# Two SwiGLU feed-forwards of a decoder layer, their products made by seven block products in place of eight

## The chip, the cores and the metric

The kernel runs on one core of a Trainium2 chip. A core has TensorE (matrix products, into PSUM), VectorE and ScalarE (element-wise work, both can read PSUM), GpSimd (element-wise work in SBUF only) and SyncE, whose queue (SP) issues nearly all of this kernel's DMA transfers. In the profile they are PE (with PEld for its weight loads), ACT for ScalarE, DVE for VectorE, POOL for GpSimd and SP. The metric is the device time of one execution in microseconds; the median of several runs is compared.

## The reference

One layer of a hybrid decoder, for 1024 tokens of a prompt and 8 sequences of 8 new tokens. Model width 1024, feed-forward width 2816, all in float32. What concerns the change are the two half-step feed-forwards, one ahead of the token mixing and one behind it:

```python
def rmsnorm(x, g):
    xf = x.astype(jnp.float32)
    y = xf * lax.rsqrt(jnp.mean(xf * xf, axis=-1, keepdims=True) + EPS)
    return (y * g.astype(jnp.float32)).astype(x.dtype)

def swiglu(x, w_in, w_out):
    gu = x @ w_in                               # (tokens, 1024) @ (1024, 5632)
    g, u = gu[..., :D_FF], gu[..., D_FF:]
    return (jax.nn.silu(g) * u) @ w_out         # (tokens, 2816) @ (2816, 1024)

def layer(x, ...):
    x = x + 0.5 * swiglu(rmsnorm(x, norm_ffn1[l]), ffn1_w_in[l], ffn1_w_out[l])
    mix, ... = token_mixing(rmsnorm(x, norm_mix[l]), ...)
    x = x + mix
    x = x + 0.5 * swiglu(rmsnorm(x, norm_ffn2[l]), ffn2_w_in[l], ffn2_w_out[l])
```

The mixing (a causal pooling branch and a Mamba-2 state-space branch, merged by gates) is not changed in what it computes. At the end a final RMS norm gives the outputs; the states of the mixer are returned too.

## The kernel before

**Layout and precision.** Activations are feature-major: a tile has 128 features on the partitions and the tokens along it. The 1088 tokens are two halves, 512 tokens (half 0) and 576 (half 1: 512 of the prompt and the 64 new ones). A PSUM bank holds 512 columns, so half 1 is worked in two pieces of 288 (`PIECES`, L33). A product in float32 is made of three passes in a reduced float format: each operand is split into a high part and the exact rest, and high x high, high x low and low x high are added up (`products`, L252). So each pair of a weight block and a k-tile is nine matmuls: three passes of 512, 288 and 288 columns.

**Weights.** `load_w` (L239) loads up to four 128x128 blocks in one transfer (tile `wraw`, four buffers), ScalarE copies them to the high part `wh` (L248), VectorE subtracts to get the low part `wl` (L249); four buffers each. These splits have a raised priority.

**A feed-forward** (`ffn`, L391) goes through the 22 hidden tiles in blocks (`FF_BLOCKS`, L35: 3, 4, 4, 4, 4, 3). For each tile of a block: the gate product (`pg`, 8 k-tiles), SiLU, the up product (`pu`), their product, and a split into hidden high and low parts (`hb`, `hs`), which stay in SBUF. Then the block's share of the output product is made for all eight output tiles (`po`), and VectorE adds half of it to x straight from PSUM (L431). In the first block the two halves are worked one after the other, so that half 1's operand may still be made while half 0 is multiplied; in the last block the output runs by parts (`ends`, L391), so that the next stage can begin on what is finished. x stays in SBUF through the feed-forward.

**Ahead of the first feed-forward** `load_x` (L443) loads x token-major, turns it on TensorE, copies it from PSUM (L466, ScalarE and VectorE in turn) and splits x times its gain at once; the RMS factors are worked out beside the first products and applied to the product's result (`rs`). Elsewhere `norm_split` (L344) makes the normalized operand: squares, a sum over the partitions on TensorE, Newton steps, a way through DRAM to spread the factors (`rstd`, L303), the product, and one split for each of the eight tiles.

**Order.** Such helpers are generators, "chains". Each `yield` says how much TensorE time should pass before its next step, and `tick` (L132) weaves due steps into the stream of products; `finish` (L128) runs one to its end. The order so traced is each instruction's priority; what is issued first on each engine and on the DMA queue is then settled ahead of time by a scheduler that takes the first ready instruction by priority.

**Buffers.** 58 activation tiles of 128x576 (`act`, L82) are shared by all stages; three big tiles, small tiles and PSUM (four banks of products, four others) are opened once for the whole kernel.

**The end.** `turn_out` (L1152) turns finished blocks of 128 tokens to token-major, with ScalarE squaring and summing (L1159); `final` (L1177) scales and stores them. The last part has 256 prompt tokens and the 64 new ones (`parts`, L1150).

## Time and profile before

| what | us |
|---|---|
| runs | 3079.87, 3076.58, 3070.76 |
| median of the runs | 3076.58 |
| span of the profiled execution | 3076.2 |
| TensorE busy in it | 3024.0 (18600 matmuls) |
| VectorE busy | 1624.1 |
| ScalarE busy | 1028.7 |
| GpSimd busy | 56.4 |
| first feed-forward, first to last product | 12.4 to 831.6 |
| second feed-forward | 2268.0 to 3061.5 |

A row of the groups reads: line of the code, engine, operation, output tile <- input tiles, shape of each, how often, then busy time in us and mean ns of one, then the idle time of the engine just before them and what ended it. A row of a timeline or of the chain reads: start in us, length in us, engine, line, operation, count. A row of windows gives the stretch, its length, the busy time (and count) of each engine, the granted TensorE clock as a share of the full one, the busy share of the DMA engines, and GB/s. Matmuls are pipelined, so the duration of one is not its pitch: the pitch is the distance from start to start in a stretch that runs without idle time.

### The profile page before, as it was taken

How to read it: one execution, taken by the hardware profiler on the slowest of the kernel's cores; microseconds unless marked ns; L12 is line 12 of the kernel's file. 1: busy time of each engine (PE TensorE's matmuls, PEld its weight loads, DVE VectorE, ACT ScalarE, POOL GpSimd, SP SyncE). 2: the span in 40 equal slices, each digit the busy share in tenths (PEclk: the TensorE clock that was granted, in tenths of full speed). 3: DMA queues.
4: the chain of work that ended last, by engine and by line, in shares of the span. 5: the costliest groups of instructions: out<-in, count | busy, mean ns of one | idle time of the engine just before them, and what ended most of it. 6: DMA issues, size and time to landing. Idle time of an engine off the chain costs nothing.

```text
span 3076.2 us, 46636 instructions
## 1 busy us (share of the span) xinstructions
PE 3024.0 (98%) x18600; PEld 2750.7 (89%) x18600; DVE 1624.1 (53%) x3331; ACT 1028.7 (33%) x1967; POOL 56.4 (2%) x170
## 2 busy tenths in 40 slices
PE   6999999999999999999999999999999999999998
PEld 5999999999888888888999989999999999999997
DVE  5533333333673897777726886977773222322225
ACT  4221212121343665434425554543442212111113
POOL 0000000000000000000001110100000000000000
PEclk8999999999999999999999999999999999999999
DMA  4211111111434333435333434244432111111112
GB/s 132 67 45 45 45 45 45 45 45 43 130 97 124 113 103 92 117 117 183 91 102 95 123 104 119 88 139 124 145 113 64 44 45 45 45 45 45 45 41 98
DMA packets 439262, 261.10 MB, mean 85 GB/s; under 512 B 21795, under 2 KB 412066, under 8 KB 439036
## 3 DMA queue, kind: packets, MB, share of 16 engines
q1 hardware_dynamic: 439028, 258.11, 28.8%
q8 instruction: 146, 2.39, 0.3%
q14 instruction: 72, 0.59, 0.1%
q10 hardware_dynamic: 16, 0.00, 0.0%
HBM read 232.31 MB, written 25.97 MB: 84 GB/s over the span
## 4 chain that ended last, share of the span: by engine, by line
PE 92%; DVE 4%; DMA 2%; ACT 1%; issue 1%; SPq 0%; POOL 0%; ACTq 0%; DVEq 0%; POOLq 0%
PE pg L140 22%; PE pu L140 20%; PE po L140 17%; PE pc L140 8%; PE pz L140 6%; PE pso L140 5%; PE pwo L140 3%; PE pbp L140 3%; PE pyd L140 2%; PE pyos L140 1%; PE pst L140 1%; DMA bsel<-in_bsel_dram 1%; PE pyo L140 1%; PE pgm L140 1%; DVE wl L249 1%
## 5 line engine op out<-in xcount | busy, mean ns | idle before, releaser
L248 ACT ACTIVATE wh<-wraw 128x512 fp32r<-128x512 f32 (+1 forms) x708 | 440.2, 623 | 1643.8 <-PE pg L140 423.7
L249 DVE TENSOR_TENSOR wl<-wraw,wh 128x512 fp32r<-128x512 f32 (+1 forms) x708 | 479.1, 679 | 651.5 <-ACT wh L248 642.0
L140 PE MATMUL pg<-hi,wh 128*128 128x288 f32 (+1 forms) x1440 | 349.3, 331 | 15.4 <-ACT wh L248 15.4
L140 PE MATMUL po<-hb,wh 128*128 128x288 f32 (+2 forms) x1600 | 348.1, 339 | 0.0
L140 PE MATMUL pg<-lo,wh 128*128 128x288 f32 (+1 forms) x1440 | 346.3, 329 | 0.4 <-DVE lo L290 0.4
L140 PE MATMUL pg<-hi,wl 128*128 128x288 f32 (+1 forms) x1440 | 345.7, 328 | 0.0
L140 PE MATMUL pu<-hi,wh 128*128 128x288 f32 (+1 forms) x1248 | 293.9, 329 | 0.1
L140 PE MATMUL pu<-hi,wl 128*128 128x288 f32 (+1 forms) x1248 | 292.3, 328 | 0.0
L140 PE MATMUL pu<-lo,wh 128*128 128x288 f32 (+1 forms) x1248 | 292.2, 327 | 0.0
L140 PEld LDWEIGHTS pg<-hi,wh 128*128 128x128 f32 x1440 | 245.4, 189 | 38.0 <-ACT wh L248 16.3
L140 PEld LDWEIGHTS po<-hb,wh 128*128 128x128 f32 x1600 | 255.8, 188 | 19.6 <-ACT hb L286 0.3
L140 PEld LDWEIGHTS pg<-lo,wh 128*128 128x128 f32 x1440 | 245.3, 189 | 21.2 <-DVE lo L290 1.1
L140 PEld LDWEIGHTS pg<-hi,wl 128*128 128x128 f32 x1440 | 245.1, 189 | 20.7 <-DVE wl L249 0.4
L140 PE MATMUL po<-hb,wl 128*128 128x288 f32 (+3 forms) x1056 | 240.4, 328 | 0.0
L140 PEld LDWEIGHTS pu<-hi,wh 128*128 128x128 f32 x1248 | 211.8, 188 | 18.6 <-ACT wh L248 0.5
L140 PEld LDWEIGHTS pu<-hi,wl 128*128 128x128 f32 x1248 | 211.7, 188 | 17.7
L140 PEld LDWEIGHTS pu<-lo,wh 128*128 128x128 f32 x1248 | 211.7, 188 | 17.5
L140 PEld LDWEIGHTS po<-hb,wl 128*128 128x128 f32 x1056 | 178.6, 188 | 15.1
L431 DVE SCALAR_TENSOR_TENSOR x<-po,x 128x288 f32<-128x288 f32 (+3 forms) x240 | 108.7, 497 | 135.2 <-PE po L140 135.0
L140 PE MATMUL pc<-hi,wh 128*128 128x288 f32 (+1 forms) x576 | 162.8, 335 | 0.6 <-ACT craw L529 0.6
L140 PE MATMUL pc<-hi,wl 128*128 128x288 f32 (+1 forms) x576 | 159.7, 329 | 0.0
L140 PE MATMUL pc<-lo,wh 128*128 128x288 f32 (+1 forms) x576 | 158.6, 329 | 0.0
(283 smaller groups left out, 4608.6 us busy)
## 6 DMA issues: line engine op xcount, KB each, us to landing
wraw<-in_w_in_dram SPq DMA_DIRECT2D x260, 256.0 KB
wraw<-in_ffn_w_in_dram SPq DMA_DIRECT2D x200, 256.0 KB
wraw<-in_ffn_w_out_dram SPq DMA_DIRECT2D x64, 256.0 KB
ab<-acsd SPq DMA_DIRECT2D x64, 256.0 KB
wraw<-in_ssd_w_out_dram SPq DMA_DIRECT2D x64, 256.0 KB
wraw<-in_ffn_w_out_dram SPq DMA_DIRECT2D x48, 192.0 KB
wraw<-in_pool_w_out_dram SPq DMA_DIRECT2D x32, 256.0 KB
wraw<-in_w_o_dram SPq DMA_DIRECT2D x32, 256.0 KB
```

Source lines behind the costliest of these rows:

```text
L140: T.matmul(out, lhsT, rhs, start=start, stop=stop)
L248: S.activation(wh, raw, AF.Copy)
L249: V.tensor_tensor(wl, raw, wh.bitcast(F32), op=ALU.subtract)
L431: V.scalar_tensor_tensor(x_[:, a:b], pt[:, : b - a], 0.5, x_[:, a:b], op0=ALU.mult, op1=ALU.add)
```

## The change

Both products of both feed-forwards are made by one level of Strassen's scheme in Winograd's form. The two operands are cut into 2x2 blocks; seven sums and differences of blocks of each are formed, seven products are made of them in place of eight, and the four blocks of the result are sums of those.

- *Blocks.* Of the activations: two groups of k-tiles by two groups of tokens (256 + 256 in half 0, 288 + 288 in half 1, `NPAIR`). Of the input weights: the k-halves (4 + 4 tiles) by gate and up columns of one hidden tile. Of the output weights: the two halves of a block's hidden tiles by two neighbouring output tiles.
- *Operands.* GpSimd forms the sums (`combine` for activations, `add` in `wino_weights`). Each of the seven is split into high and low parts: `split_x` for activations (one activation tile holds both parts, 28 tiles for an operand of one half), `parts` for weights. The weights are loaded as before but combined anew for each use.
- *Accumulation.* `PRODUCTS` gives the order and the PSUM bank (0, 1 or 2) of the seven products; some add on to a bank that has been read in between. The result is put together on the way out of PSUM: by ScalarE, VectorE and GpSimd in `ffn_in` and `ffn_out`.
- *Order of the feed-forward.* All 22 hidden tiles are made first and stored to DRAM (`hdram`), the first three (`N_APART`) for each half by itself. Then, block by block (6, 6, 6, 4), the hidden tiles are loaded back, combined, and multiplied; x is stored ahead and loaded back for the sum.
- *Start.* `load_x` works out the RMS factors from the token-major x and makes the normalized, combined operand itself; all copies of turned blocks go to VectorE.
- *Buffers.* Raw weights 6 (4 before), split weights 3 (4), PSUM in the feed-forwards 6 banks of products and 2 others; pools for the stages open and close with each of the two feed-forwards and the mixer.
- *End.* The last part has half 1's five token blocks.

The diff, cut to its core (removed lines only where they aren't told above):

```diff
+NPAIR = (256, 288)
+FF_BLOCKS = (6, 6, 6, 4)
+N_RAW, N_W = 6, 3
+N_X2, N_TMP, N_S, N_PDF = 12, 11, 4, 6
+N_APART = 3
+PRODUCTS = (("1", 0), ("2", 1), ("6", 0), ("5", 2), ("7", 0), ("3", 2), ("4", 0))
...
+    def wino_weights(w, ka, kb, nk, ca, cb, raws=None):
+        if raws is None:
+            raws = wino_raw(w, ka, kb, nk, ca, cb)
+        a11, a12, a21, a22 = raws
+        def add(a, b, op, name):
+            t = stage["p"].tile([P, 4 * P], F32, tag="wsum", bufs=N_S, name=nm(name))[:, : nk * P]
+            with tc.high_priority(hp[0]):
+                G.tensor_tensor(t, a, b, op=op)
+            return t
+        def parts(a):
+            wh, wl = (sp.tile([P, 4 * P], F32R, tag=t, bufs=N_W, name=nm(t))[:, : nk * P] for t in ("wh", "wl"))
+            with tc.high_priority(hp[0]):
+                S.activation(wh, a, AF.Copy)
+                V.tensor_tensor(wl, a, wh.bitcast(F32), op=ALU.subtract)
+            return wh.rearrange("p (k c) -> p k c", c=P), wl.rearrange("p (k c) -> p k c", c=P)
+        yield parts(a11)
+        yield parts(a12)
+        s1 = add(a21, a22, ALU.add, "s1")
+        s2 = add(s1, a11, ALU.subtract, "s2")
+        yield parts(s2)
+        yield parts(s1)
+        s3 = add(a11, a21, ALU.subtract, "s3")
+        yield parts(s3)
+        s4 = add(a12, s2, ALU.subtract, "s4")
+        yield parts(s4)
+        yield parts(a22)
+    def wino(weights, nk, xs, after):
+        banks = [[None] * 3 for _ in xs]
+        for (p, b), (wh, wl) in zip(PRODUCTS, weights):
+            for i, (h, X) in enumerate(xs):
+                n = NPAIR[h]
+                new = banks[i][b] is None
+                if new:
+                    banks[i][b] = psum("pd", "pw" + p)
+                out = banks[i][b][:, :n]
+                for k in range(nk):
+                    x = X[p][k]
+                    for j, (W, c) in enumerate(((wh, 0), (wh, n), (wl, 0))):
+                        mm(out, W[:, k, :], x[:, c : c + n], start=new and k == 0 and j == 0, stop=k == nk - 1 and j == 2, free=True)
+                after(p, i, banks[i])
+                tick()
+    def split_x(src, h):
+        n = NPAIR[h]
+        t = act((P, 576), F32R, "X")
+        S.activation(t[:, :n], src, AF.Copy)
+        V.tensor_tensor(t[:, n : 2 * n], src, t[:, :n].bitcast(F32), op=ALU.subtract)
+        return t
+    def combine(h, pairs, X, pace=None):
...
+        for p, _ in PRODUCTS:
+            X[p] = []
+            for i, (a, b) in enumerate(pairs):
+                a1, a2, b1, b2 = a[:, :n], a[:, n : 2 * n], b[:, :n], b[:, n : 2 * n]
+                if p == "6":
+                    sub(a2, a2, a1)
+                    t2[i] = tmp(n, "t2")
+                    sub(t2[i], b2, a2)
+                elif p == "7":
+                    sub(a1, t2[i], a1)
+                elif p == "4":
+                    sub(b1, b1, t2[i])
+                X[p].append(split_x({"1": a1, "2": b1, "6": t2[i], "5": a2, "7": a1, "3": b2, "4": b1}[p], h))
+                if pace is not None:
+                    yield pace
+    def ffn_in(wi, ff, xs, hd, raws=None):
...
+            if p == "1":
+                out[i] = o = {"g": x2(name="g"), "t1": tmp(n)}
+                S.copy(o["t1"], A)
+                return
...
+            if p == "2":
+                V.tensor_tensor(g1, B, o["t1"], op=ALU.add)
+                S.activation(g1, g1, AF.Silu)
+            elif p == "6":
+                o["t2"] = tmp(n)
+                S.copy(o["t2"], A)
+            elif p == "5":
+                o["t5"] = tmp(n)
+                S.copy(o["t5"], C)
+            elif p == "7":
+                V.tensor_tensor(o["t5"], A, o["t5"], op=ALU.add)
+            elif p == "3":
+                V.tensor_tensor(g2, C, o["t2"], op=ALU.add)
+                S.activation(g2, g2, AF.Silu)
+            else:
+                V.tensor_tensor(g1, g1, A, op=ALU.mult)
+                G.tensor_tensor(g2, g2, o["t5"], op=ALU.mult)
+                dma(hd[h][ff], o["g"][:, : 2 * n])
+        wino(wino_weights(wi, 0, 4, 4, ff * P, FF + ff * P, raws), 4, xs, after)
+    def ffn_out(wo, k0, nk, m, xs, xt):
...
+            if p in "167":
+                t = tmp(n)
+                S.activation(t, A, AF.Copy, scale=0.5)
+                o = {"1": a1, "6": a2, "7": b2}[p]
+                G.tensor_tensor(o, o, t, op=ALU.add)
+            else:
+                src, o = {"2": (B, a1), "5": (C, b2), "3": (C, a2), "4": (A, b1)}[p]
+                V.scalar_tensor_tensor(o, src, 0.5, o, op0=ALU.mult, op1=ALU.add)
+        wino(wino_weights(wo, k0, k0 + nk, nk, m * P, (m + 1) * P), nk, xs, after)
+    def ffn(wi, wo, X, hd, before, after, half=None, raws=None):
...
+        for h in HALVES:
+            before(h)
+            for i, ff in enumerate(order[:N_APART]):
+                ffn_in(wi, ff, [(h, X[h])], hd, raws if h == 0 and i == 0 else None)
+        for ff in order[N_APART:]:
+            ffn_in(wi, ff, [(h, X[h]) for h in HALVES], hd)
...
+        for bi, nb in enumerate(FF_BLOCKS):
...
+                for k in range(nb):
+                    t = act((P, 576), name="hr")
+                    dma(t[:, :N], hd[h][b0 + k])
...
+            last = bi == len(FF_BLOCKS) - 1
+            for grp in ((0,), (1,)) if last else (HALVES,):
+                for m in range(0, KD, 2):
+                    ffn_out(wo, b0, nk, m, [(h, H[h]) for h in grp], xt)
...
-    parts = (prompt[:6], prompt[6:] + [sample])
+    parts = (prompt[:4], prompt[4:] + [sample])
```

More of the change, by code (lines that the diff above doesn't have):

```diff
@@ L218, in load_consts @@
             dma(bsel3[i * 32 : (i + 1) * 32, :], c_bsel[0:32, 0:4])
-        for t in xdtp:
-            G.memset(t, 0.0)
         yield 12
@@ new lines, in load_x @@
+        for m in range(KD):
+            dma(xspill[h][m], x[m][:, :N])
+        yield 0.5
+        pairs = []
+        for i in range(4):
+            ab = []
+            for k in (i, 4 + i):
+                t = act((P, 576), name="xn")
+                V.scalar_tensor_tensor(t[:, :N], x[k][:, :N], cols[:, i_g1 + k : i_g1 + k + 1], r[:, :N], op0=ALU.mult, op1=ALU.mult)
+                ab.append(t)
+            pairs.append(ab)
+            yield 0.5
+        yield from combine(h, pairs, X1[h], 0.35)
```

281 lines of the change are left out of this document (154 added, 127 removed).

## The prediction

> **What bounds the kernel now.** I read the page first (engine totals and slices), then the chain of waits in order of time, then windows over the feed-forwards, then groups of instructions.
>
> ```profile
> span 3076.2 us, 46636 instructions
> PE 3024.0 (98%) x18600; PEld 2750.7 (89%) x18600; DVE 1624.1 (53%) x3331; ACT 1028.7 (33%) x1967; POOL 56.4 (2%) x170
> DVE  5533333333673897777726886977773222322225
> GB/s 132 67 45 45 45 45 45 45 45 43 130 97 124 113 103 92 117 117 183 91 102 95 123 104 119 88 139 124 145 113 64 44 45 45 45 45 45 45 41 98
> ...
> PE 92%; DVE 4%; DMA 2%; ACT 1%; issue 1%; SPq 0%; POOL 0%; ACTq 0%; DVEq 0%; POOLq 0%
> ```
>
> TensorE is the bound: 98% of the span, 92% of the chain. The feed-forwards are the ends of the span, where VectorE is at 3 tenths and DMA at 45 GB/s; the mixer is the middle. The next rows are windows of TensorE alone: from the first product of the first feed-forward to its first output product, and most of the second one.
>
> ```profile
> 12.40:114.90 102.50, 85.80 (x499) 0.90 0.36 97
> 114.90:795.00 680.10, 680.10 (x4107) 1.00 0.16 45
> 2340.00:3019.00 679.00, 679.00 (x4104) 1.00 0.16 46
> ```
>
> Away from the start there is no gap to remove, so the only gain is fewer microseconds of matmul. A busy time is no throughput, so I take the pitch from pieces of the chain (start, length, count):
>
> ```profile
> 366.00 11.92 PE pg L140 x72
> 1165.26 16.34 PE pz L140 x72
> 1605.39 25.60 PE pbp L140 x192
> ```
>
> One 128x128 weight block against the 1088 tokens is 512+288+288 columns: 72 matmuls in 11.92 us, 165.6 ns each. The first half's z projection is all 512 columns, 16.34/72 = 226.9 ns; the second half's pooling product is all 288, 25.60/192 = 133.3 ns. The line through them is 0.418 ns a column.
>
> **The products.** Before, one feed-forward is (44x8 + 8x22) = 528 weight blocks x 3 split passes x 3 pieces = 4752 matmuls, x 165.6 ns = 787 us. After, the input product takes 22 tiles x 7 products x 4 k x 3 passes = 1848 pairs of one 256-column and one 288-column matmul, the output 4 x 7 x 11 x 3 = 924 pairs: 2772 pairs, 5544 matmuls. More instructions, 7/8 of the columns. The price of 256 columns is the question: the line gives 119.9 ns. A stretch that alternates 512 and 256, and 128-column ones, are the other rows:
>
> ```profile
> 3025.30 0.87 PE L140 MATMUL po<-hb,wh 128*128 128x512 f32 x4
> 3026.01 0.51 PE L140 MATMUL po<-hb,wl 128*128 128x512 f32 x2
> 3026.36 0.87 PE L140 MATMUL po<-hb,wh 128*128 128x512 f32 x4
> ...
> 1162.42 1.05 PE L140 MATMUL pyo<-Cf,hst 128*128 128x128 f32 x8
> 1163.31 0.94 PE L140 MATMUL pyd<-ab,xdtp 128*128 128x128 f32 x7
> ```
>
> Six matmuls, three of each width, start within 1.06 us, so 256 costs 353.3 - 226.9 = 126.4 ns. Eight of 128 columns take 0.89 us, 111 ns, far over their 66 ns by the line: a floor that does not depend on the columns. 256 columns lie just above it. A pair is thus 244.6 (floor), 253.2 (line) or 259.7 ns (mixed stretch): 678, 702 or 720 us per feed-forward, a gain for both of 217, 170 or 134 us. I take the line, since uniform streams are the nearest.
> [...]
>
> **What is added beside TensorE, steady state.** Groups of VectorE, ScalarE and GpSimd (count, busy, mean ns), and the last stores in the timeline:
>
> ```profile
> L249 DVE TENSOR_TENSOR wl<-wraw,wh 128x512 fp32r<-128x512 f32 x660 | 452.6, 688 | 623.3 <-ACT wh L248 613.8 <-PE ph0T L144 2.5 <-DMA wraw<-in_pool_w_group_dram 2.5
> L249 DVE TENSOR_TENSOR wl<-wraw,wh 128x384 fp32r<-128x384 f32 x48 | 26.4, 552 | 28.2 <-ACT wh L248 28.2
> L364 DVE TENSOR_TENSOR g<-pu,g 128x288 f32<-128x288 f32 x44 | 17.9, 449 | 6.0 <-PE pu L140 6.0
> L248 ACT ACTIVATE wh<-wraw 128x512 fp32r<-128x512 f32 x660 | 415.0, 630 | 1541.8 <-PE pg L140 401.1 <-PE po L140 351.8 <-PE pu L140 322.8
> L368 ACT ACTIVATE g<-pg 128x288 f32<-128x288 f32 x44 | 15.5, 407 | 0.0
> L220 POOL MEMSET xdtp<- 128x1024 f32 x2 | 1.8, 952 | 0.0
> L735 POOL COPY cst<-crs 128x24 f32<-128x24 f32 x24 | 7.7, 319 | 0.7 <-ACT crs L531 0.7
> L729 POOL COPY crs<-hist 128x24 f32<-128x24 f32 x24 | 21.3, 899 | 226.7 <-DVE hist L769 169.1 <-DVE ct L743 54.0 <-DVE rsm L300 3.5
> ...
> 3061.45 11.84 SPq L1196 DMA_DIRECT2D out_dram<-xtok  x18
> ```
>
> An input tile takes TensorE 84 x 253.2 = 21.3 us. VectorE needs 7 splits x 0.69 + 8 reads of PSUM x 0.43 = 8.3 us; ScalarE 7 x 0.63 + 10 x 0.41 = 8.5. Both fit. GpSimd has no two-input row. Call p its add of 512 columns: below by the memset, 0.48 us; above by three times VectorE's 0.69, 2.1 (the two copies of 24 columns lie a factor of three apart); I take 1.0, their geometric middle. A tile needs 4p + 2x0.53p = 5 us, an output group of two column tiles (k=3) 6.2p against TensorE's 16.0: cost 0 under that cover.
> Weights and traffic: the same weights, plus hidden tiles out and back, 12 MB each per feed-forward; input tiles then move 1.6 MB in 21 us, 75 GB/s, under the 183 GB/s that one slice reaches: 0. A hidden tile's store waits on SP for GpSimd's last product, and the next tile's weight loads queue behind it; six raw buffers are a tile and a half ahead, so 0; without that, 1 MB at 183 is 5.7 us a tile. SP issues some 120 transfers more per feed-forward (44 hidden tiles out, 44 in, 16 of x each way); at 11.84/18 = 0.66 us an issue that is 79 us of an otherwise idle queue.
>
> **The seams** are where the gain can go back: every operand must now be combined and split seven times before its products. Rows for them (grouped instructions, windows of all engines, the end of the timeline):
>
> ```profile
> L466 DVE COPY x<-ptx x36: 214/285/292, 9.2 to 65.8; 128x128 f32<-128x128 f32 x32, 128x64 f32<-128x64 f32 x4
> L290 DVE SCALAR_TENSOR_TENSOR lo<-xn,cols,hi x32: 744/782/821, 830.1 to 2304.8; 128x512 fp32r<-128x512 f32 x16, 128x576 fp32r<-128x576 f32 x16
> L314 DVE TENSOR_TENSOR ssq<-ssq,sq 128x576 f32<-128x576 f32 x33 | 24.9, 755 | 4.5 <-ACT sq L313 3.3
> ...
> 12.40:831.60 819.20, 802.50 (x4829) 728.59 (x4827) 321.39 (x631) 184.28 (x317) 0.44 (x4) 0.99 0.20 58
> 2200.00:2300.00 100.00, 96.21 (x596) 90.11 (x595) 68.47 (x132) 44.49 (x71) 0.00 (x0) 0.95 0.43 130
> 2268.00:3061.50 793.50, 793.49 (x4820) 724.54 (x4819) 249.53 (x467) 165.26 (x305) 0.00 (x0) 1.00 0.17 50
> 3061.50:3076.20 14.70, 1.69 (x14) 1.15 (x12) 7.43 (x25) 6.66 (x14) 0.00 (x0) 0.64 0.82 303
> ...
> 3064.39 0.58 ACT L1159 ACTIVATE junk<-ptf 128x512 f32<-128x512 f32 x1
> 3064.87 0.19 ACT L1159 ACTIVATION_READ_ACCUMULATOR junk<-ptf 128x1 f32 x1
> ```
>
> VectorE's 0.688 and 0.552 us put a split of 256 columns at 0.42 us and of 288 at 0.45.
> - *Start.* The first three tiles run one half after the other. Before the second half's products VectorE must do 68 copies x 0.26 (all on it now) = 17.7, 16 gains x 0.78 = 12.5, 28 splits x (0.42 + 0.45) = 24.4, 21 weight splits x 0.69 = 14.4, 12 reads of PSUM = 5, small ones 5: 79 us from 9.2 on, so 88 us where TensorE has 30 to do. The second half's 252 matmuls of 288 add 33.6: 122 us, with 63.8 of products done, 58 lost. Before, the first feed-forward ended at 831.6, 45 over its 787. Net 13, and 4 for the waits of the combining chain: 17 (0 if the chains mesh; 47 if GpSimd's 30 us there lie in the path).
> - *From input to output product* (twice): hidden tiles need activation slots that the first operand holds (56 of 58), so their 3.3 MB (18 us at 183 GB/s) start when the last tile's first product releases eight of them, 18 us before its end. Then 42 splits: VectorE 18.3 + 7.3 for the first group against TensorE's 16. I take 8 each (0 to 25).
> - *Between output blocks* (six): the last group of one block and the first of the next are 32 us; VectorE has 18.3 + 2 x 7.3 = 33. I take 3 each, 18 (0 to 60).
> - *Last block*, per half: a group is 42 matmuls, 5.0 to 5.6 us; GpSimd has 3.6p, VectorE 7 x 0.42 + 4 x 0.43 = 4.7, and a product lasts 0.7 us with three split buffers. 6 each, 12 (6 to 40).
> - *Second feed-forward's start*: while the first half's three tiles run (252 x 119.9 = 30 us), VectorE must add 7 squares (5.3), 8 gains (6.5), 28 splits (12.6), small ones 2.5, on top of the tiles' 19.4: 46 us, 16 late; 4 more for the first half's splits, in a stretch where VectorE is at 68 of 100. 20 (5 to 40).
> - *End*: five token blocks follow the last product, not three: two more squares (0.77 each with their read), four more stores (0.66 each): 5 (3 to 10).
> - *Mixer*: three split-weight buffers, not four; its two padding tiles and its PSUM now open at its start: 8 (0 to 25).
> Sum 17 + 16 + 18 + 12 + 20 + 5 + 8 = 96 back. Against the profiled execution's 3076.2 us (the runs' median is 3076.58, so it stands for them): 3076 - 170 + 96 = **3002 us**.
>
> **Rivals.**
> 1. *GpSimd becomes the bound: slower.* Place: the output product. Its 3.6p outlasts a last-block group's 5.0 us from p = 1.4, and 6.2p a normal group's 16.0 from 2.6. At p = 2.9: 12 x 2.0 + 8 x 5.4 = 67 per feed-forward, 3002 - 12 + 134 = 3124; it turns to slower near 2.7. Against it: 2.1 is my upper bound. For it: no two-input row exists, and a strided copy of 24 columns took 0.90.
> 2. *GpSimd and VectorE hold each other up: slower.* If an operation of GpSimd cannot run beside one of VectorE that reads two SBUF tiles, their times add. Steady tiles bear it (5 + 4.8 of 21.3), seams don't: GpSimd's work there (p = 1.0) is 31 us at the start (12 adds, 32 subtractions of 0.53, 3 products), 20 at the second start, per output change 25 beside 25 of such splits in 32 us, so 16 beyond the 3 above (96 in all), 12 in last blocks, 24 at the two phase changes: 183 more if all adds up, 3185; it turns to slower at 74, or 40% of it. Against it: much of that work can move ahead of need. The page's GpSimd row (56 us in all) shows no such pair.
> [...]
> 3. *The seams are hidden*: only ends and mixer cost, some 30 us: 2936. For it: VectorE and ScalarE are near 30% busy in the feed-forwards; the instruction order can be filled from ready work.
> 4. *No gain in the pitch*: if each matmul took the mean 165 ns of today's weight loads, 5544 would cost 915 us and the time would be 3330. The 133 ns row speaks against it.
> 5. *Gain and seams cancel*: the pitch at 259.7 and seams at 134: 3076.
>
> **The numbers.** Runs lie within 0.3% of each other, some 9 us, so 3067 to 3085 is "no change". Chances: forecast, 2965 to 3067, 0.53; hidden seams 0.20; cancelled 0.05; GpSimd slow 0.07; engines holding each other up 0.13; pitch 0.02. Faster 0.73, same 0.05, slower 0.22. Range 2915 to 3120: it leaves out the far ends of rivals 1, 2 and 4, and the best case (gain 217, no seams). Of the forecast alone: 2965 to 3040.
>
> **What would show it.** Right: 256 columns at about 120 ns in the chain and pairs at 253; input stretches with TensorE without idle time, some 21.3 us a tile; idle TensorE released by VectorE's splits near 20 to 90 us, near the second start and at block changes; VectorE's busy time up by some 140 us in the second feed-forward (22 x 8.3 + 16 groups x 7 + 91 of splits, against 249.5). Wrong: idle TensorE all along the output product released by GpSimd; weight adds well over 1 us; VectorE's splits longer than 0.42 where GpSimd runs; gaps in the middle of input tiles. Wrong, too, if the clock (0.90 in the gappy first window, 1.00 after) falls at each seam, since a pitch then grows where I only counted waits.

## The result, and the profile after

| | us |
|---|---|
| before, median of 4 runs | 3076.09 |
| after, median of 4 runs | 3160.57 |
| ratio, 95% interval | 1.0281 (1.0266 to 1.0295) |
| profiled execution of after: run, span | 3163.61, 3161.8 |

The change made the kernel 2.8% slower; the forecast was 2.4% faster. The totals and three rows of the slices on the page of the kernel after:

```profile
span 3161.8 us, 54565 instructions
PE 2925.8 (93%) x20182; PEld 2761.4 (87%) x20182; DVE 2096.4 (66%) x4076; ACT 1412.5 (45%) x3097; POOL 948.9 (30%) x1050
...
PE   6799999887899999999999999999978999987887
...
POOL 4633334676700000000001110100055333357665
PEclk7899999888899999999999999999988999999998
```

TensorE's busy time fell by 98 us, from 3024.0 to 2925.8, but it no longer fills the span: 236 us are idle in place of 52. The idle slices are the starts and the output products, and there GpSimd is at 4 to 7 tenths. In the first feed-forward they are also the slices with a lowered granted clock; in the second one's output product all slices but the last still show 9 tenths, and the lower clock is seen only in the windows below. Windows of TensorE by stage, in which the boundaries are the starts of the first matmuls of each stage (columns: stretch, length, TensorE busy and matmuls, granted clock, DMA share, GB/s):

```profile
31.90:147.70 115.80, 89.29 (x555) 0.79 0.35 106
147.70:561.50 413.80, 403.71 (x3196) 0.99 0.27 88
561.50:634.30 72.80, 68.04 (x505) 0.92 0.39 125
634.30:801.20 166.90, 134.74 (x1010) 0.89 0.22 69
801.20:874.90 73.70, 57.04 (x346) 0.88 0.39 120
2327.40:2419.90 92.50, 75.28 (x516) 0.83 0.30 91
2419.90:2833.20 413.30, 403.27 (x3194) 1.00 0.27 87
2833.20:2905.30 72.10, 67.27 (x505) 0.93 0.39 126
2905.30:3072.30 167.00, 134.67 (x1010) 0.89 0.23 69
3072.30:3144.50 72.20, 58.17 (x389) 0.91 0.25 81
...
200.00:300.00 100.00, 100.00 (x796) 100.00 (x795) 39.63 (x73) 37.23 (x80) 32.24 (x29) 1.00 0.27 84
```

The last row, with all engines (PE, PEld, DVE, ACT, POOL), is a stretch inside the input product without idle time: 796 matmuls in 100 us, 125.6 ns each, 251.2 a pair. A feed-forward's 5544 matmuls are thus worth 696.5 us in place of 787, which is 181 us gained by both. Each stage's length less its own matmuls at that pitch (504 at a start and in the first block, 3192 in the joint input tiles, 1008 in blocks two and three, 336 in the last) is what the stage lost. Beside the same losses before (12.4 us ahead of the first product, 32.2 in the first feed-forward, 6.5 in the second, 14.7 at the end, and 1436.4 us between the two, which is this row of the kernel before):

```profile
831.60:2268.00 1436.40, 1421.40 (x8918) 1291.76 (x8917) 1041.62 (x2200) 666.79 (x1319) 53.25 (x156) 0.99 0.40 116
```

| seam | lost after, us | more than before | forecast |
|---|---|---|---|
| first start: 31.9 ahead of it, 115.8 - 63.3 | 84.4 | 39.8 | 17 |
| input to output product: joint tiles 12.8 and 12.3, first block 9.5 and 8.8 | 43.4 | 43.4 | 16 |
| into blocks two and three, both feed-forwards: 40.3 + 40.4 | 80.7 | 80.7 | 12 |
| last block and the change into it: 73.7 - 42.2, 72.2 - 42.2 | 61.5 | 61.5 | 6 + 12 |
| mixer: 2327.4 - 874.9, against 1436.4 | | 16.1 | 8 |
| second start: 92.5 - 63.3, less 6.5 | 29.2 | 22.7 | 20 |
| end | 17.3 | 2.6 | 5 |
| sum | | 266.8 | 96 |

181 gained and 266.8 given back are 85.8 us slower, and the spans differ by 85.6 (the stages cover the whole span, so the two have to agree). The seams cost 170.8 us more than forecast, of which 139.6 lie in the three rows of the output product; the products gave 11 more than forecast. (A loss here holds both waiting and matmuls that ran slower than the undisturbed pitch.)

The waits of TensorE, the two largest (line waited for, us in total, times, longest), are both for split weights of `parts`, which ScalarE copies and VectorE subtracts:

```profile
PE pw L163 <- ACT wh L415: 68.4, 15, 9.7
PE pw L163 <- DVE wl L416: 55.6, 32, 5.0
```

What keeps these two engines busy is seen in the chain of waits, here at the entry to the second block of the second feed-forward (first its shares by line, then start and length of each piece):

```profile
by line: DVE X L462 40.5%; PE pw L163 33.7%; POOL t L472 11.0%; POOL x L538 5.0%; DVE x L541 3.5%; issue 3.5%; DVE wl L416 2.4%; ACT X L461 1.1%; POOLq L538 0.0%
...
2905.13 2.60 POOL t L472 x3
...
2911.19 5.81 DVE X L462 x7
...
2917.17 4.00 DVE X L462 x7
...
2925.57 4.64 PE pw L163 x19
```

In 40 us TensorE holds a third of the chain. Most of the rest is VectorE's splits of the block's operand (`X`, L462), at 0.83 us each in the first of the two rows of seven, and GpSimd's subtractions in `combine` (L472). The same place in the first feed-forward: the spread of L462's durations (min/median/max in ns), and then the groups of VectorE and GpSimd around the entry to the third block, 720 to 753 us (count, busy us, mean ns).

```profile
L462 DVE TENSOR_TENSOR X<-hr,X x8: 615/993/1015, 638.7 to 645.2; 128x256 fp32r<-128x256 f32 x4, 128x288 fp32r<-128x288 f32 x4
...
L462 DVE TENSOR_TENSOR X<-hr,X 128x256 fp32r<-128x256 f32 x14 | 11.4, 812 | 0.0
L462 DVE TENSOR_TENSOR X<-hr,X 128x288 fp32r<-128x288 f32 x14 | 11.0, 788 | 0.0
L541 DVE SCALAR_TENSOR_TENSOR x<-pw,x 128x288 f32<-128x288 f32 x5 | 2.2, 448 | 0.7 <-PE pw L163 0.7
...
L472 POOL TENSOR_TENSOR hr<-hr,t 128x256 f32<-128x256 f32 x3 | 2.7, 903 | 0.0
L472 POOL TENSOR_TENSOR hr<-t,hr 128x256 f32<-128x256 f32 x3 | 2.7, 902 | 0.0
```

The same subtraction of 256 columns that the forecast put at 0.42 us takes 0.81 us in the mean; of the eight splits in the first row, four of each width, the median is 0.99. VectorE's update of x from PSUM (L541), one operand in PSUM and one in SBUF, still takes 0.45 us for 288 columns between them. Of VectorE's rows shown here, only those that read two SBUF tiles are stretched.

The trace says the same instruction by instruction. Of the 256 updates of x from PSUM (L541) in this kernel, the 146 that had a tensor operation of GpSimd beside them all along took 0.41 to 0.46 us, like the others. Of the 210 operand splits of 256 columns in this kernel, the 88 that had a tensor operation of GpSimd beside them for less than half of their length took 0.41 to 0.43 us, every one. The 97 that had one beside them all along took 0.56 to 1.53, in the mean 0.91.

The second thing to see is when the splits are made. The splits that VectorE made for the second block during the last group of the first one (617.0 to 634.3), from the timeline:

```profile
618.06 3.82 DVE L462 TENSOR_TENSOR X<-hr,X 128x256 fp32r<-128x256 f32 x5
...
622.60 1.54 DVE L462 TENSOR_TENSOR X<-hr,X 128x288 fp32r<-128x288 f32 x2
...
624.43 0.44 DVE L462 TENSOR_TENSOR X<-hr,X 128x288 fp32r<-128x288 f32 x1
...
625.27 3.47 DVE L462 TENSOR_TENSOR X<-hr,X 128x256 fp32r<-128x256 f32 x4
...
632.86 0.57 DVE L462 TENSOR_TENSOR X<-t,X 128x256 fp32r<-128x256 f32 x1 [1.08 <-ACT X L461]
...
633.69 0.73 DVE L462 TENSOR_TENSOR X<-t,X 128x288 fp32r<-128x288 f32 x1
```

14 of 42. A block's operand holds 42 of the 58 activation slots and the next block's hidden tiles 12 more, so the first slots come free when the last group has used them. The slots alone do not make it 14, though: the version without subtractions, below, has the same slots and made 25 ahead. The other 28 splits fall into the first group of the new block, which took 34.8 us (from its first matmul to the next group's) against 15.9 for an undisturbed one.

### The profile page after: what moved, and what is told of

It is laid out like the page before. It is cut to its first block, busy times and chain, and to the rows that moved or that the text cites. A ratio compares the mean times of both kernels' runs of the same rounds, so it can differ in the third digit from the quotient of the medians.

```text
span 3161.8 us, 54565 instructions
## 1 busy us (share of the span) xinstructions
PE 2925.8 (93%) x20182; PEld 2761.4 (87%) x20182; DVE 2096.4 (66%) x4076; ACT 1412.5 (45%) x3097; POOL 948.9 (30%) x1050
## 5 line engine op out<-in xcount | busy, mean ns | idle before, releaser
L163 PE MATMUL pw<-X,wh 128*128 128x256 f32 (+1 forms) x7392 | 1453.6, 296 | 118.0 <-ACT wh L415 68.4
L163 PEld LDWEIGHTS pw<-X,wh 128*128 128x128 f32 x7392 | 1200.7, 196 | 135.0 <-ACT wh L415 73.2
L163 PE MATMUL pw<-X,wl 128*128 128x256 f32 (+1 forms) x3696 | 1084.9, 295 | 55.7 <-DVE wl L416 55.6
L163 PEld LDWEIGHTS pw<-X,wl 128*128 128x128 f32 x3696 | 718.6, 195 | 66.0 <-DVE wl L416 64.9
L268 ACT ACTIVATE wh<-wraw 128x512 fp32r<-128x512 f32 x396 | 248.3, 629 | 479.0 <-PE pz L163 109.0
L416 DVE TENSOR_TENSOR wl<-s,wh 128x512 fp32r<-128x512 f32 (+2 forms) x360 | 256.7, 718 | 241.0 <-ACT wh L415 233.9
L269 DVE TENSOR_TENSOR wl<-wraw,wh 128x512 fp32r<-128x512 f32 x396 | 274.1, 694 | 212.4 <-ACT wh L268 197.4
L415 ACT ACTIVATE wh<-s 128x512 fp32r<-128x512 f32 (+2 forms) x360 | 202.7, 564 | 344.2 <-PE pw L163 303.9
L409 POOL TENSOR_TENSOR s<-wraw,wraw 128x512 f32<-128x512 f32 (+2 forms) x180 | 213.2, 1184 | 328.3 <-DVE wl L416 271.7
L416 DVE TENSOR_TENSOR wl<-wraw,wh 128x512 fp32r<-128x512 f32 (+2 forms) x270 | 197.7, 735 | 124.6 <-ACT wh L415 119.7
L462 DVE TENSOR_TENSOR X<-hr,X 128x256 fp32r<-128x256 f32 (+1 forms) x264 | 182.9, 752 | 1.7 <-ACT X L461 1.7
L541 DVE SCALAR_TENSOR_TENSOR x<-pw,x 128x256 f32<-128x256 f32 (+1 forms) x256 | 110.3, 435 | 61.1 <-PE pw L163 50.3
L409 POOL TENSOR_TENSOR s<-wraw,s 128x512 f32<-128x512 f32 (+2 forms) x90 | 110.2, 1224 | 72.7 <-issue 68.3
L409 POOL TENSOR_TENSOR s<-s,wraw 128x512 f32<-128x512 f32 (+2 forms) x90 | 103.9, 1155 | 83.2 <-issue 65.3
L936 DVE SCALAR_TENSOR_TENSOR ct<-craw,cwh,ct 128x512 f32<-128x512 f32 x144 | 107.8, 748 | 22.7 <-ACT ct L934 21.9
```

The lines of the kernel that those rows point to most:

```text
L163: T.matmul(out, lhsT, rhs, start=start, stop=stop, skip_group_check=free)
L268: S.activation(wh, raw, AF.Copy)
L269: V.tensor_tensor(wl, raw, wh.bitcast(F32), op=ALU.subtract)
L409: G.tensor_tensor(t, a, b, op=op)
L415: S.activation(wh, a, AF.Copy)
L416: V.tensor_tensor(wl, a, wh.bitcast(F32), op=ALU.subtract)
```

## The experiments

Four theories. **Exclusion**: GpSimd's subtractions and VectorE's two-operand splits get in each other's way, whoever needs the results. **Chain**: products wait because the values come late through GpSimd's queue (subtractions behind sums of weights and updates of x); in the kernel after ScalarE waited 44.4 us in 45 waits for the subtraction `t` before copies of the operand. **Amount**: VectorE has too many splits to make in a seam, wherever the subtractions run. **Order**: the splits are only in a wrong order for the first products. The first four kernels have one run each, and the kernel before ran once beside them, at 3075.05 us; the others have four runs each and a ratio to the kernel before.

**Without the subtractions.** `combine`'s subtractions are left out (all operands are then made of uncombined blocks); every copy and split stays.

```diff
-            G.tensor_tensor(out, a, b, op=ALU.subtract)
+            pass
...
-                    t2[i] = tmp(n, "t2")
+                    t2[i] = b2
```

> All subtractions of activation blocks on GpSimd are left out (the seven operands are then plain blocks, so the products are of wrong operands; every split and matmul stays). Three theories of the 19 us that the first group of an output block loses (35 us against 16). Exclusion: a GpSimd operation and a VectorE operation that reads two SBUF tiles hold each other up, so splits of 0.43 us take 0.7 to 1.0. Chain: ScalarE and VectorE stand in their queues behind splits whose input GpSimd has not made yet. Amount: 42 splits are too many for VectorE whatever GpSimd does. Exclusion and chain both expect splits of hidden tiles at 0.43 us, first groups at 18 to 22 us and a time near 3040 (six block changes x 15, 20 at the two starts). Amount expects first groups over 30 us and a time over 3120.

Measured: 3051.15 us, 109 us under the kernel after. The first group of block two took 19.3 us, against 34.8, and 54 of the 109 us came back in blocks two and three of the two feed-forwards.

**With subtractions that nobody reads.** As above, but GpSimd makes each of them into a scratch tile.

```diff
-            pass
+            G.tensor_tensor(tmp(n, "ts"), a, b, op=ALU.subtract)
```

> The same subtractions are made on GpSimd, but into scratch tiles that nobody reads; the splits take the plain blocks, as in the run without them. GpSimd's work is all there, nobody waits for its result. Exclusion expects splits still at 0.7 to 1.0 us, first groups at 26 us or more and a time over 3090. Chain expects the time of the run without the subtractions, near 3040, however long a split is.

Measured: 3176.36 us, and a first group of 34.6 us. No split takes one of these results. They still hold something up, though: a subtraction reads a hidden tile, and that tile's slot comes free only behind it. So ScalarE's copies of the operand waited for GpSimd here too (first row below: us in total, times, longest). VectorE shows whether that set the time. The second row is the change into block two with all engines, and VectorE was busy in all 42 us of it:

```profile
ACT X L461 <- POOL ts L472: 47.5, 15, 9.8
...
619.00:661.00 42.00, 26.70 (x169) 25.41 (x168) 42.00 (x62) 20.32 (x59) 35.21 (x37) 0.81 0.22 70
```

**Subtractions on VectorE.**

```diff
-            G.tensor_tensor(out, a, b, op=ALU.subtract)
+            V.tensor_tensor(out, a, b, op=ALU.subtract)
```

> The subtractions of activation blocks move from GpSimd to VectorE; all is computed. A subtraction should take 0.43 us in place of 0.95. VectorE gets 24 x 0.43 = 10 us more per block change, GpSimd loses 23. Exclusion expects splits near 0.43 to 0.5 us and first groups at 22 to 28 us: 3080 to 3110. Chain expects about the same or less, 3060 to 3100. Amount expects 10 us more at each of the six changes and both starts: 3220 or more.

Measured: 3124.72 us, 36 under the kernel after, with a first group of 27.9 us. The time lies in none of the expected ranges. The groups of VectorE's splits without the subtractions, with unread ones, and with those on VectorE, one fence for each kernel:

```profile
L462 DVE TENSOR_TENSOR X<-hr,X 128x288 fp32r<-128x288 f32 x154 | 94.7, 615 | 0.0
L462 DVE TENSOR_TENSOR X<-hr,X 128x256 fp32r<-128x256 f32 x154 | 79.6, 517 | 1.7 <-ACT X L461 1.7
```

```profile
L462 DVE TENSOR_TENSOR X<-hr,X 128x288 fp32r<-128x288 f32 x154 | 133.8, 869 | 0.0
L462 DVE TENSOR_TENSOR X<-hr,X 128x256 fp32r<-128x256 f32 x154 | 120.0, 779 | 2.9 <-ACT X L461 2.9
```

```profile
L462 DVE TENSOR_TENSOR X<-hr,X 128x288 fp32r<-128x288 f32 x132 | 77.7, 588 | 0.0
L462 DVE TENSOR_TENSOR X<-hr,X 128x256 fp32r<-128x256 f32 x132 | 63.6, 482 | 0.3 <-ACT X L461 0.2
```

The first two kernels differ only in that GpSimd works, and no product takes a result of that work; yet the splits are 0.25 us longer and the time is 125 us longer. At the change into block two VectorE had no idle time to lose to late copies, so there it is the longer splits that cost: Exclusion is shown. How much of the 125 us is waiting for slots elsewhere was not taken apart. Chain alone falls: taking the products' need of the values away gained nothing. The third adds that the price is not all in the place. Of the 109 us that the subtractions cost, 36 go when VectorE makes them itself and 73 stay. I read these as Amount, work on an engine that has no room in a seam; but the copies wait for the subtractions in this version as well, and no version made unread subtractions on VectorE, so that part is argued. Its windows of blocks two and three in the first feed-forward (columns as above, all engines), first without the subtractions, then with them on VectorE:

```profile
613.10:752.50 139.40, 131.67 (x1010) 129.21 (x1009) 105.17 (x206) 68.33 (x179) 87.28 (x80) 0.99 0.27 83
```

```profile
624.70:780.30 155.60, 134.06 (x1010) 130.96 (x1010) 118.04 (x252) 72.41 (x186) 83.36 (x80) 0.93 0.24 74
```

139.4 and 155.6 us against 166.9 for the kernel after and 126.6 of matmuls: 12.8, 29.0 and 40.3 lost. The granted clock goes with the losses: 0.99, 0.93 and 0.89. At 0.89 the 1008 matmuls are busy for 134.7 us, 8.1 more than at the undisturbed pitch, but that is not all slower work: at 0.99 they are busy for 131.7 already, since the busy time counts the last matmul before each gap in full (one of 256 columns lasts 0.28 us in the trace, at a pitch of 0.12). By their starts in the trace of the kernel after, 46 of the 1008 matmuls began 0.15 to 0.3 us behind the one before, which is 4.4 us over their pitch, and 13 longer pauses make 35.5 us. So about a ninth of what is lost there is slower matmuls, and the rest is waiting.

**Splits traced product by product** in the first group of a block, in place of all at once ahead of it.

```diff
-            for _ in range(7 * nk):
-                for h in HALVES:
-                    next(H[h]["gen"])
+            step(HALVES, 2 * nk)
...
+            if ahead:
+                ahead()
```

> The operand's splits are no longer traced all ahead of a block's first product: those of the first two products are, those of each later product just before the product two earlier. The work is the same. If the loss is one of order (the weights' splits of the first products queue behind all 42 operand splits), first groups fall to 22 us and the time to near 3080. If it is GpSimd and VectorE holding each other up, the sum of their work stays and the first groups stay at 30 us or more, 3130 to 3160.

Measured: 3161.17 us, no difference, and a first group of 35.3 us. Order falls.

**The output product plain again**, the input product as in the kernel after.

```diff
-                for m in range(0, KD, 2):
-                    ffn_out(wo, b0, nk, m, [(h, H[h]) for h in grp], xt)
+                for m in range(KD):
+                    po = dense(wo, b0, nb, m * P, [H[h] for h in grp], "pd", "po")
+                    for h, pts in zip(grp, po):
+                        x_ = xt[h][m]
+                        for pt, (a, b) in zip(pts, PIECES[h]):
+                            V.scalar_tensor_tensor(x_[:, a:b], pt[:, : b - a], 0.5, x_[:, a:b], op0=ALU.mult, op1=ALU.add)
```

> One part of the change alone: the input product stays in seven block products with the hidden tiles through DRAM; the output product is the plain one again (hidden tiles loaded back, split once each, three passes over 512+288+288 columns, added to x from PSUM by VectorE). In the changed kernel an output phase takes 312 us; plain it is 1584 matmuls x 165.6 ns = 262. Theory now: the output product's seven-fold combining and splitting costs more than its matmuls save (block changes and last blocks), the input product saves. Expected 3160 - 2 x 50 = 3060, 3045 to 3075. Rival: the phase change through DRAM is the cost, whatever follows: then only the block changes' part comes back and the time is 3080 or more.

Measured: 3052.44 us against 3076.72 before, ratio 0.9917 (0.9901 to 0.9934). Half of the change is a gain, the other half more than eats it: giving up an eighth of the output product's columns saves 108 us.

**The same with the subtractions on VectorE**, and **the same with ScalarE sharing the copies of the turned x**:

```diff
-            G.tensor_tensor(out, a, b, op=ALU.subtract)
+            V.tensor_tensor(out, a, b, op=ALU.subtract)
...
-                    V.tensor_copy(x[q * 4 + k][:, c0 : c0 + c], pt[:, k * P : k * P + c])
+                    (V.tensor_copy if k % 2 else S.copy)(x[q * 4 + k][:, c0 : c0 + c], pt[:, k * P : k * P + c])
```

> The same, and the subtractions of the input operand's blocks on VectorE in place of GpSimd. They are only at the two starts now. If GpSimd and VectorE hold each other up there, the starts lose some 6 us: 3054. If VectorE's amount of work decides there, the starts gain 14 subtractions x 0.43 of VectorE each way: 3060 to 3075.

> The same as the one before, and the copies of the turned x from PSUM shared by ScalarE and VectorE in turn, as before the change. VectorE has 9 us less before the first tiles. If VectorE's amount sets the start, 6 to 9 us less than the run before; if the start hangs on the arrival of x and on the chain of factors, no change.

Measured: 0.9905 (0.989 to 0.992), 3047.29 us; and with the shared copies 0.9907 (0.9892 to 0.9921), 3047.78 us. Neither differs from the one before it by more than the intervals. What was left lay at the starts; the next three kernels begin from the first of these two.

**Fewer tile pairs apart** (`N_APART` 1 and 2 in place of 3):

> The version with the plain output product and VectorE's subtractions (3047 us), with one tile pair per half taken apart at the start of a feed-forward instead of three (N_APART 3 to 1). Each tile pair taken apart needs its seven weight tiles copied and split twice, once for each half. Theory Load: at the starts VectorE is the bound (42 splits wl of 0.82 to 0.99 us in 110 us, VectorE 90% busy); two pairs fewer save 14 splits of 0.9 us = 12.6 us of VectorE at each start, some 10 us of the time, so about 3027 us. Theory Cover: the pairs of half 1 are what TensorE does while half 2's X are made (24+24+8 splits and subtractions, about 30 us of VectorE); one pair is 10.6 us of TensorE instead of 32, so it stands some 10 us longer at one or both starts, 3050 to 3065 us. Taken: 3047 to 3060, Cover eating what Load gives.

> The same with two tile pairs per half taken apart (N_APART 3 to 2). Theory Load: 7 splits of 0.9 us fewer at each start, about 3037 us. Theory Cover: 3047 to 3055 us. Taken: 3044.

Measured: 0.9923 (0.9907 to 0.9939) with one, 0.9899 (0.9883 to 0.9916) with two, against 0.9905 with three. The intervals overlap, so these two versions do not decide between load and cover.

**Without the sums of weights**: a block is used in place of each sum.

```diff
-            t = stage["p"].tile([P, 4 * P], F32, tag="wsum", bufs=N_S, name=nm(name))[:, : nk * P]
-            with tc.high_priority(hp[0]):
-                G.tensor_tensor(t, a, b, op=op)
-            return t
+            return a
```

> The version with the plain output product and VectorE's subtractions (3047 us), with the four sums of weight blocks on GpSimd left out: one of the two blocks is used in place of each sum, so the product is not the reference's. The copy and the split of each stay. What this tells: whether what is left of GpSimd (100 to 200 sums of 1.35 to 1.8 us) still costs anything. Theory Exclusion: the splits wl of 0.82 to 0.99 us at the starts come back to about 0.69 us as in the mixer, 41 x 0.2 = 8 us at each start, so about 3031 us, and no difference in the rest of the input phases, where TensorE has no idle time. Theory Amount: the starts are set by the number of X and weight tiles that VectorE has to make, not by their length, and the time stays within 3042 to 3050 us. Taken: 3033 us.

Measured: 0.9836 (0.9822 to 0.9851), 3024.21 us; the difference of the ratios, 0.0069, is 21 us. The weights' splits on VectorE in the first start, 30 to 142 us, with the sums on GpSimd and then without them:

```profile
L416 DVE TENSOR_TENSOR wl<-s,wh 128x512 fp32r<-128x512 f32 x23 | 21.7, 953 | 3.0 <-ACT wh L415 3.0
L416 DVE TENSOR_TENSOR wl<-wraw,wh 128x512 fp32r<-128x512 f32 x18 | 14.7, 815 | 1.8 <-ACT wh L415 1.3
```

```profile
L413 DVE TENSOR_TENSOR wl<-wraw,wh 128x512 fp32r<-128x512 f32 x44 | 30.3, 689 | 10.7 <-ACT wh L412 9.8
```

0.89 us in the mean with the sums, 0.69 without: Exclusion again, with other operations in another stage. The 41 splits are 8 us longer in all at this start. This version also takes away the wait for a sum, and no version made sums that nobody reads, so the rest of the 21 us is not shown to be Exclusion. In the steady input tiles, 200 to 500 us, the same splits took 0.692 us with the sums and TensorE had no idle time: there the two engines have room to miss each other. In the kernel after, 85 of the 99 splits in that stretch had no tensor operation of GpSimd beside them, the other 14 for at most four tenths of their length, and all 99 took 0.69 us.

**The first three tile pairs of each half plain again.** They need no sums of weights, 4 splits of weights in place of 7, and only the four uncombined blocks of x; the combined ones are made (on VectorE) while the plain pairs run, and the 19 joint tiles stay in seven products.

```diff
+    def firsts(h, pairs, X, pace):
+        for p in "12A3":
+            for a, b in pairs:
+                X[p].append(split_x({"1": a1, "2": b1, "3": b2, "A": a2}[p], h, h == 1 and p == "A"))
...
+    def rest(h, X, pace):
+        for p in "6574":
...
+            if h == 1:
+                rs = [start(rest(0, X[0], 0.9)), start(rest(1, X[1], 0.9), 16 * 0.9)]
             for i, ff in enumerate(order[:N_APART]):
-                ffn_in(wi, ff, [(h, X[h])], hd, raws if h == 0 and i == 0 else None)
+                ffn_in_plain(wi, ff, h, X[h], hd, raws if h == 0 and i == 0 else None)
```

> The version with the plain output product and VectorE's subtractions (3047 us), in which the three tile pairs per half that open a feed-forward are plain products again: they need no sums of weights and no combined X, so they can start when four of the eight X blocks have been split, with 4 splits of weights a pair in place of 7. The other combinations of both halves are made while these plain pairs run; the 19 joint pairs stay in Strassen's form. Theory (VectorE's load and GpSimd's sums at the starts are what is lost there: 47 us at the first start and some 35 at the second, by gaps between first and joint pairs of 110 and 94 us against 63 us of work): six plain pairs take 72 us in place of 63, 9 more at each start, and the idle time falls to some 10 us at each, so 3047 - (47 + 35) + 2 x (9 + 10) = about 3003 us. Rival: VectorE is as busy as before (its 112 splits and 32 subtractions stay) and TensorE waits for it at the joint pairs in place of the first ones, 3035 to 3055 us.

> The same with two plain pairs per half in place of three. Plain pairs cost 3 us less at each start, and cover 24 us less of VectorE's work. By the theory 2998 to 3010 us where the cover still holds; by the rival a few us more than with three. Taken: 3006 us.

Measured: with three pairs 2997.21 us against 3077.82 before, ratio 0.9745 (0.9729 to 0.9762); with two 3000.23 us, 0.9752 (0.9738 to 0.9767). The page's totals and windows of all engines, of the version with three: the first start, the joint tiles with their seven products, and the second start.

```profile
PE 2926.7 (98%) x19798; PEld 2743.5 (92%) x19798; DVE 1756.2 (59%) x3660; ACT 1211.6 (40%) x2477; POOL 316.2 (11%) x398
...
27.80:140.00 112.20, 103.50 (x774) 101.41 (x775) 81.30 (x211) 54.57 (x141) 11.64 (x9) 0.93 0.41 123
140.00:524.30 384.30, 384.30 (x3047) 384.11 (x3046) 156.99 (x286) 149.41 (x315) 118.31 (x105) 1.00 0.27 87
...
2215.00:2320.00 105.00, 102.28 (x796) 101.83 (x795) 71.91 (x163) 46.70 (x107) 10.71 (x8) 0.98 0.37 113
```

TensorE's busy time is that of the kernel after to within a microsecond, 2926.7, but it is 98% of a shorter span. It is not the same work: at the undisturbed pitch the plain output product and the plain first pairs are some 39 us more per feed-forward, so the kernel after spent as much busy time on 78 us less of it. This version beats both kernels: 2.5% under the one before. What changed is that nothing of the combining is needed before TensorE has other work, and that GpSimd is near idle (11.64 us in 112) while VectorE splits.

## Why the prediction was wrong

**The products: right.** Pairs were taken at 253.2 ns and measured 251.2; the gain was 170 and measured 181. The uniform rows decided rightly over the mixed stretch (259.7), and the rival without a gain in pitch fell.

**Steady state: right.** Input tiles run without idle time: of the 413.8 us in the first feed-forward 401 are products at the pitch, and most of the rest is one wait, at the change to the output product. GpSimd's add of 512 columns, taken at 1.0 us, took 1.35 in its largest group (L409: 100 of them, 135.3 us), inside its bounds. By that it is not the bound, as the first rival needed 2.7 and GpSimd is at most 7 tenths busy.

**Between output blocks: the step that failed.** I put VectorE's 33 us against 32 us of TensorE, over the last group of a block and the first of the next, and took 3 us each. Blocks two and three lost 20 us each. Three things were wrong with the balance. It let the work spread evenly over both groups, where only 14 of the 42 splits were made ahead of the boundary. It took a split at 0.42 to 0.45 us, where GpSimd made it 0.79 to 0.81. And it let matmuls keep their pitch, where the clock fell to 0.89; that is the smallest, about 2 us a block. Without the subtractions a block loses 6.4 us and with them 20.2, so 13.8 of the 17 us that the forecast missed come with GpSimd's subtractions; with those on VectorE a block loses 14.5. Why, with the subtractions on VectorE, again only 14 splits were made ahead (19 with unread ones on GpSimd, 25 without any) was not settled.

**The last block and the change into it**: 18 forecast, 61.5 measured; **input to output**: 16, 43.4; **first start**: 17, 39.8, near the 47 that I gave for GpSimd's work lying in the path. All three terms are sums of VectorE's work at undisturbed durations, like the one above, but GpSimd's subtractions are not the main cost in all of them. Without the subtractions the last blocks still lost 25.4 and 20.3 us, 45.7 of the 61.5, and the way from input to output 25.6 of the 43.4. The last block of the first feed-forward in that version, where 42.2 us are products:

```profile
752.50:820.10 67.60, 56.00 (x347) 0.92 0.43 131
```

What holds up the last block there was not found, so the cause of that term stays open; the loss is gone, with all the other seams of the output, when that product is plain. For the starts the runs show that VectorE's work and GpSimd's sums are the cost: without the sums of weights 21 us come back, and with plain first pairs 50 (3047.29 to 2997.21 us).

**Second start, mixer, end**: 20, 8 and 5 forecast, 22.7, 16.1 and 2.6 measured. Sizes were off by few us; but second start and mixer together lost 38.8 where 28 was forecast, and with plain first pairs the mixer's part came back: 1438.3 us from the first feed-forward's last product (789.5) to the second one's first (2227.8), against 1436.4 before and 1452.5 after.

**The rivals.** The second one, GpSimd and VectorE holding each other up, was what happened, and I gave it 0.13. That VectorE's splits get longer beside GpSimd's work is shown (0.41 us alone, 0.91 in the mean beside it, at 256 columns), not that the times add in full; its size was right for a reason that isn't quite its own. It gave 3185 if all adds up and the kernel took 3161, but the subtractions' place accounts for 36 us of that and the weights' sums for some 21, measured in another version. The kernel with the subtractions on VectorE still took 3125, above the kernel before, so the sign would have turned without that place too. The case that I lacked is this one: seams too full for VectorE even where it is less disturbed (GpSimd still made the weights' sums and the updates of x there). The fourth rival's price was too low by its own terms: 3330 leaves out the 96 us of seams. The third rival, hidden seams, fell in the kernel as changed, and its argument, that the engines are near 30% busy, is the average that says nothing about a seam.

**The signs that I listed.** Right: pairs at 253, input stretches without idle time, waits for VectorE's splits at the named places. VectorE's busy time in the second feed-forward was to rise by 140 us, from 249.5 to 390; it was 491, and by the means of its groups some 90 us of the surplus are stretched splits. Wrong signs that came: splits longer than 0.42 where GpSimd runs, weight adds over 1 us, and a falling clock at the seams.

## What to carry to other kernels

A scheme that trades matmul time for operand work pays where each operand is used often and its making can be spread: the input operand of a half, 28 split tiles used 22 times, gained; the output operand of a block, 42 split tiles used in four groups of 16 us, lost more than its eighth. Price a seam by what can be made before it (slots that are free, results that exist), and not by the mean load around it. And do not count GpSimd as a free second VectorE while VectorE reads two SBUF tiles (here a split of 256 columns took 0.91 us in the mean beside it, 0.41 alone): give such work to one engine, or to a stretch in which the other has slack, and open each phase with work that needs none of it.

## What the runs showed of the hardware

At the change into block two GpSimd and VectorE at once did less than twice the work of one. In 11.05 us (637.59 to 648.64, the stretch with the median of 0.99 us a split) GpSimd made 12 subtractions and VectorE 12 splits, six of each width on either engine, so 0.92 us for one of each. A split takes 0.41 us for 256 columns and 0.45 for 288 without a tensor operation of GpSimd beside it (the means of 76 and 66 in the kernel after), and GpSimd's product of 256 columns 0.737 us in the version with plain first pairs:

```profile
L548 POOL TENSOR_TENSOR g<-g,t 128x256 f32<-128x256 f32 x38 | 28.0, 737 | 242.4 <-ACT g L545 242.4
```

If a subtraction alone is as long as that product, and longer by the columns at 288, the 12 subtractions are an estimated 9.4 us and the splits 5.2, in turn 14.6. Side by side the pair saved about a quarter of that by this estimate; had the two taken strict turns, it would have saved nothing. The longer delay fell on VectorE, whose splits took more than twice their time (the median 0.99 us); GpSimd's subtractions took 0.90 to 1.01 us, against an estimated 0.74 and 0.83.

The granted clock fell with gaps in TensorE's work as short as those of a block change: in blocks two and three of the first feed-forward 0.89 over 167 us with 40 us lost, where the longest wait was 9.6 us, and 0.99 over 139 us with 13 lost in the version without the subtractions; 1.00 in the input product between 200 and 300 us, with none. Behind the last gap at the change into block two, which ended at 654.5 us, the matmuls ran slower for some 3.8 us: the granted clock was 0.50 from 646.3 to 658.2 us and 1.00 from 658.5 to 662. In the rows below, after that gap, three start in 0.64 us (654.85 to 655.49), and later three in 0.35 (658.53 to 658.88):

```profile
654.85 0.63 PE L163 MATMUL pw<-X,wh 128*128 128x256 f32 x2
...
655.49 0.63 PE L163 MATMUL pw<-X,wh 128*128 128x256 f32 x2
...
658.53 0.40 PE L163 MATMUL pw<-X,wh 128*128 128x256 f32 x2
...
658.88 0.40 PE L163 MATMUL pw<-X,wh 128*128 128x256 f32 x2
```

In these two blocks the gaps were thus paid for twice, by the wait and by the matmuls behind it, though the second part is small: 4.4 us of 40.
